# The split of a gate-up group's last pair on GpSimd, its products by lower parts at the end, and one more pair of FFN 1's second group as seven products

## The chip, the cores and the metric

The kernel runs on one core of a Trainium2 chip. The metric is the device time of one launch in microseconds (us). The engines in the text: TensorE (PE; its weight loads, which overlap the matmuls, are PEld), VectorE (DVE), ScalarE (ACT), GpSimd (POOL) and SyncE (SP), which issues most of the DMAs.

## The reference, cut to what matters

One encoder layer on x (256 tokens x 2048): two SwiGLU feed-forward networks with a mixer between them, all in float32. Each FFN is

```
def swiglu(x, w_gate_up, w_down):
    gate, up = jnp.split(x @ w_gate_up, 2, axis=-1)
    return (jax.nn.silu(gate) * up) @ w_down
```

with w_gate_up 2048 x 11264 and w_down 5632 x 2048. The change touches only the first product of both FFNs, `x @ w_gate_up`.

## The kernel before, in words

**Two parts of a number.** Every float32 operand is split in an upper part h (a cast to the matmul type, on ACT, line 176) and a lower part l = value - h (a subtraction, on DVE unless another engine is given, line 177). A product is three matmuls, h by h, h by l and l by h, each with a stationary 128x128 piece of x and a moving 128x512 piece of the weights (`three`, line 443).

**Groups and pairs.** The gate-up product runs over 11 groups g (512 gate columns and 512 up columns); a group runs over 8 pairs u of 128 rows of x. Its result is four PSUM banks c[m][n] (m: half of the tokens, n: gate or up). A plain pair is 8 products, so 24 matmuls. A pair in `MIXED_IN` is done as seven products, 21 matmuls, by a scheme of sums: sums of the blocks of x are made once, and sums of the blocks of w for every group (`splits`, lines 985 and 986, with a DMA that adds one part of w to another, `add_second`, line 148, on GpSimd's queue). The first of its four blocks is split ahead by `prepare`, as h1 and l1. The seven products go to four more banks p1, p5, p6, p7 besides the c banks. In groups 2 to 10 of both networks the pairs 2, 4, 5 and 6 are done so; in group 1, a network's second, only 4 and 5 in FFN 1 and 2, 4 and 5 in FFN 2; in group 0 none.

**The boundary.** At the end of a group the p banks have to be added into the c banks. `boundary` does it while PE works on the last pair, 7: ACT copies p1 (L1193), and then DVE does a row of eight instructions: L1194 adds to c[0][0], L1195 and L1196 take in p6 and p7, L1197 adds to c[1][0], L1200 and L1201 lead to c[0][1], L1203 and L1204 to c[1][1]. PE's products of pair 7 for a bank come behind the addition into that bank; the banks' order is (0,0), (1,0), (0,1), (1,1). p6 is made in pair 6, whose seven products are in the order p1, c[0][0], p5, p7, p6, c[1][0], c[0][1].

**What sets the order.** The whole stage is written out by hand (`manual_schedule`): each engine takes its instructions in the order of the code, and waits at semaphores. `first_pairs` does pairs 0 and 1, `pair_ahead` pairs 2 to 5 (the splits of pair u+1 stand ahead of the products of pair u), and the loop at the end of `ffn` pairs 6 and 7. `units` does silu(gate)*up of the group that has ended (L1110, L1115), turns it on PE (L1135) and splits the result. Weights come by SP into five buffers; a buffer is loaded anew when its last split is done (`load_next`). In the kernel before GpSimd makes the lower parts of the next group's pair 0 (`boundary(g, gated.splits(g + 1, 0, nc.gpsimd))`), besides the adding DMAs.

In the names of the trace `xt` is x in its two parts, `xs` the sums of its blocks, `raw` the weights as they come, `pa` and `pb` the PSUM banks (c[0][.], p1, p5 are pa; c[1][.], p6, p7 are pb), and `z` and `s` two rooms of 128x512.

## Time and profile before

| | |
|---|---|
| median of three runs | 1807.68 us (1807.27 to 1808.6) |
| the profiled execution's own time | 1807.96 us |
| its span, first to last instruction | 1806.1 us |
| granted TensorE clock | 0.999 |
| PE busy | 1794.5 us (99%), 8368 matmuls |
| DVE busy | 1618.9 us (90%) |
| ACT busy | 1130.3 us (63%) |
| POOL busy | 214.8 us (12%) |

The profile's rows give, for an instruction or a run of like ones, the start from the span's begin, the duration, engine, line, operation, what it writes and reads, and in brackets the idle time before it with what ended it. A matmul's start is recorded and its end is modelled, so matmuls that follow each other overlap in the rows; their rate is read from start to start. One of a group's windows, by the times of its rows, is 172.56 to 214.36 us: from the first matmul of FFN 1's pair 7 in group 3 to that in group 4.

### The profile page before, as it was taken

What the parts mean: (1) busy time and instruction counts of PE and PEld (TensorE: products, weight loads), DVE (VectorE), ACT (ScalarE), POOL (GpSimd) and SP (SyncE); (2) the same over time, 40 slices, a digit from 0 to 9 for tenths busy, and PEclk for the clock granted to TensorE, in tenths of its full rate; (3) what the DMA queues carried; (4) which work ended last, traced back from release to release, by engine and by line L of the source; (5) the groups of instructions that cost most, each with busy time, mean ns of one, the idle gap of its engine ahead of it and who ended that gap; (6) DMA issues with size and microseconds to landing.
All of it is one profiled execution on the core that took longest, in us unless ns stands there. A gap on an engine that the chain in (4) does not pass through costs nothing.

```text
span 1806.1 us, 23876 instructions
## 1 busy us (share of the span) xinstructions
PE 1794.5 (99%) x8368; PEld 1491.2 (83%) x8368; DVE 1618.9 (90%) x2114; ACT 1130.3 (63%) x1487; POOL 214.8 (12%) x194
## 2 busy tenths in 40 slices
PE   9999999999999999999999999999999999999998
PEld 7888888888888888888889888888888888888886
DVE  6999999888999999888888888898999988899997
ACT  7566666655656667566667666556666566566663
POOL 0022211111000100000000000011111222000010
PEclk9999999999999999999999999999999999999999
DMA  9788988887799996954555767889888888699994
GB/s 370 232 253 278 285 280 255 257 248 217 249 328 305 309 285 244 293 157 166 177 168 170 253 200 273 246 239 277 279 269 276 256 249 256 188 318 339 277 315 165
DMA packets 128023, 460.63 MB, mean 255 GB/s; under 512 B 14352, under 2 KB 17168, under 8 KB 126368
## 3 DMA queue, kind: packets, MB, share of 16 engines
q1 hardware_dynamic: 109152, 391.18, 60.5%
q0 software_dynamic: 18608, 67.68, 20.6%
q8 instruction: 65, 1.06, 0.2%
q14 instruction: 54, 0.44, 0.1%
q10 hardware_dynamic: 144, 0.26, 0.0%
HBM read 444.38 MB, written 14.68 MB: 254 GB/s over the span
## 4 chain that ended last, share of the span: by engine, by line
PE 94%; DVE 3%; DMA 1%; ACT 1%; issue 1%; SPq 0%; POOL 0%; DVEq 0%; ACTq 0%
PE pa L443 44%; PE pb L443 38%; PE pa L315 6%; PE pa L320 3%; DVE l L177 1%; DMA raw<-in_w_mix_in_dram 1%; PE pb L1766 1%; PE pb L1135 1%; PE pa L1135 1%; PE pa L369 0%; PE pa L368 0%; PE pa L367 0%; PE pb L2065 0%; ACT xt L227 0%; ACT h L176 0%
## 5 line engine op out<-in xcount | busy, mean ns | idle before, releaser
L176 ACT CAST h<-raw 128x1024 fp32r<-128x1024 f32 (+1 forms) x849 | 831.3, 1009 | 431.6 <-PE pb L443 145.1
L177 DVE TENSOR_TENSOR l<-raw,h 128x1024 fp32r<-128x1024 f32 (+1 forms) x813 | 920.9, 1165 | 105.1 <-ACT h L176 86.8
L443 PE MATMUL pa<-h,xt 128*128 128x512 f32 x1198 | 420.6, 392 | 0.2 <-DVE xt L232 0.2
L443 PE MATMUL pb<-h,xt 128*128 128x512 f32 x1044 | 372.9, 391 | 0.4 <-DVE pb L1197 0.4
L443 PEld LDWEIGHTS pa<-h,xt 128*128 128x128 f32 x1198 | 225.0, 188 | 48.9 <-DVE xt L232 0.6
L443 PEld LDWEIGHTS pb<-h,xt 128*128 128x128 f32 x1044 | 195.9, 188 | 46.6 <-DVE pb L1204 4.0
L443 PE MATMUL pa<-l,xt 128*128 128x512 f32 x599 | 233.7, 390 | 0.6 <-DVE l L177 0.6
L443 PE MATMUL pb<-l,xt 128*128 128x512 f32 x522 | 203.3, 389 | 0.0
L443 PE MATMUL pb<-h,ht 128*128 128x512 f32 x428 | 151.2, 389 | 0.0
L443 PE MATMUL pa<-h,ht 128*128 128x512 f32 x428 | 151.1, 389 | 0.0
L148 POOL DMA_DIRECT2D raw<-in_w_ffn_gate_up_dram x77 | 67.2, 872 | 679.9 <-DVE l L177 623.8
L443 PEld LDWEIGHTS pa<-l,xt 128*128 128x128 f32 x599 | 112.6, 188 | 23.4 <-DVE l L177 1.3
L443 PE MATMUL pa<-h,xs 128*128 128x512 f32 x328 | 117.2, 389 | 0.0
L443 PE MATMUL pb<-h,xs 128*128 128x512 f32 x328 | 114.3, 389 | 0.0
L443 PEld LDWEIGHTS pb<-l,xt 128*128 128x128 f32 x522 | 98.1, 188 | 18.9
L315 PE MATMUL pa<-xt,h 128*128 128x512 f32 x448 | 109.9, 393 | 0.0
L315 PEld LDWEIGHTS pa<-xt,h 128*128 128x128 f32 x448 | 81.5, 188 | 15.3
L443 PEld LDWEIGHTS pa<-h,ht 128*128 128x128 f32 x428 | 80.4, 188 | 16.6
L443 PEld LDWEIGHTS pb<-h,ht 128*128 128x128 f32 x428 | 80.3, 188 | 16.6
L177 POOL TENSOR_TENSOR l<-raw,h 128x1024 fp32r<-128x1024 f32 x36 | 91.5, 2725 | 0.0
L443 PE MATMUL pa<-l,ht 128*128 128x512 f32 x214 | 83.3, 389 | 0.0
L443 PE MATMUL pb<-l,ht 128*128 128x512 f32 x214 | 83.3, 389 | 0.0
(341 smaller groups left out, 2592.4 us busy)
## 6 DMA issues: line engine op xcount, KB each, us to landing
raw<-in_w_ffn_gate_up_dram SPq DMA_DIRECT2D x350, 512.0 KB, 6.3
raw<-in_w_ffn_down_dram SPq DMA_DIRECT2D x176, 512.0 KB, 8.5
raw<-in_w_mix_in_dram SPq DMA_DIRECT2D x94, 512.0 KB, 4.8
raw<-in_w_ffn_gate_up_dram POOLq DMA_DIRECT2D x77, 512.0 KB, 8.4
raw<-in_w_ffn_down_dram POOLq DMA_DIRECT2D x42, 512.0 KB, 8.8
ht<-away SPq DMA_DIRECT2D x24, 512.0 KB, 10.7
raw<-in_w_mix_out_dram SPq DMA_DIRECT2D x24, 512.0 KB, 5.6
away<-ht SPq DMA_DIRECT2D x16, 512.0 KB, 7.4
```

The lines of the kernel that those rows point to most:

```text
L148: nc.gpsimd.dma_start(raw[:, 0:1024], src[:, 512:1536], accum_op=ALU.add)
L176: nc.scalar.copy(hi, src)
L177: by.tensor_tensor(lo, src, hi.bitcast(F32), ALU.subtract)
L315: nc.tensor.matmul(slot[f], weights(hs, kk, f), xcol(xt, k), start=(k == 0), stop=(k == KT - 1))
L320: nc.tensor.matmul(slot[f][:, 0:T], weights(ls, kk, f), xcol(xt, kh * 8 + kk, 0), start=False, stop=False,)
L443: nc.tensor.matmul(self.bank(at), lhs, rhs, start=(n == 1), stop=n in (ends, self.of[at]), skip_group_check=n > ends,)
L1135: nc.tensor.transpose(bank[:, o : o + P], zs[m][:, k * P : (k + 1) * P], ident)
L1766: nc.tensor.matmul(dst, left[a], right[b], start=first and i == 0, stop=last and i == 2)
```

## The change

The boundary's last pair is taken in another way. Until now a bank got all of its six matmuls of pair 7 (two rows of blocks, three matmuls each) before the next bank. Now (`take_parted`) a bank gets the four that use upper parts of the weights, and the eight that use lower parts, two for each bank, come at the very end (`lower`). The row of eight DVE instructions keeps its order, with new line numbers: L1193 is L1259, L1194 to L1197 are L1260 to L1263, L1200 and L1201 are L1266 and L1267, L1203 and L1204 are L1269 and L1270; L443 is L447, L985 and L986 are L1001 and L1002, L1110 and L1115 are L1176 and L1181.

GpSimd makes the lower parts of pair 7, behind a copy of one column (L1316) that waits for pair 6's last lower part, and the lower parts of the first blocks of the next group's pairs 4 and 5. DVE makes those of the next group's pair 0 again, behind the row of additions, and the first half of pair 1 then. The `prepare` of the next group's pair 2 moves from behind pair 7's splits to pair 5. In `units` DVE reads the turned bank in place of ACT's copy. In FFN 1's group 1 pair 6 is done as seven products too. A set `FIVE_IN` of groups with five such pairs is empty, so the code for it does nothing.

```diff
     def sums_of(u, w, also=None):
         also = u if also is None else also
         nc.vector.tensor_tensor(
-            w[:, S3::2, :], u[:, 0, :].rearrange("p (m t) -> p m t", m=2), u[:, :, P:T], ALU.subtract
+            w[:, S3::2, :], u[:, 0, :].rearrange("p (m t) -> p m t", m=2), also[:, :, P:T], ALU.subtract
         )
...
+    FIVE_IN = ()
...
-            some = MIXED_IN[1:3] if opened else MIXED_IN[:3]
+            some = MIXED_IN[1:] if opened else MIXED_IN[:3]
...
-        def prepare(self, g, u):
+        def prepare(self, g, u, by=nc.vector):
...
-            split_act(h, l, raw[:, 0:512])
+            split_act(h, l, raw[:, 0:512], by)
...
+        def take_parted(self, g, u):
+
+            (h0, l0), (h1, l1) = self.split_of.pop((g, u))
...
+            def upper(m, n):
+                for k in range(2):
+                    at, ah, al, h, _ = parts(m, n, k)
+                    self.some_of(at, (ah, h), (al, h))
+
+            def lower():
+                for k in range(2):
+                    for n in range(2):
+                        for m in range(2):
+                            at, ah, _, _, l = parts(m, n, k)
+                            self.some_of(at, (ah, l))
+
+            return upper, lower
...
             def boundary(g, ahead):
...
-                rest_of = gated.take(g, last)
-
-                def bank(m, n):
-                    for k in range(2):
-                        rest_of[4 * k + 2 * m + n]()
+                bank, lower = gated.take_parted(g, last)
...
                 bank(1, 1)
+                lower()
                 some(ahead, 2)
...
-            def first_pairs(g, waiting):
+            def first_pairs(g, waiting, ahead):
...
+                if ahead:
+                    some(waiting, 2)
+                    gated.prepare(g, sevens[1], nc.gpsimd)
+                    some(ahead, 1)
...
             def pair_ahead(g, u):
...
                 for one in gated.take(g, u):
                     one()
+                if u == last - 2 and g < NG - 1:
+                    gated.prepare(g + 1, MIXED_IN[0])
                 for _ in ahead:
                     pass
+                if u == last - 2:
+                    done = gated.split_of[g, last - 1][-1][1]
+                    nc.gpsimd.tensor_copy(warm[:, 2:3], done[:, 0:1].bitcast(F32))
...
-                    some(gated.splits(g, last), 2)
-                    if g < NG - 1:
-                        gated.prepare(g + 1, MIXED_IN[0])
+                    some(gated.splits(g, last, nc.gpsimd), 2)
                     for one in gated.take(g, last - 1):
                         one()
-                    boundary(g, gated.splits(g + 1, 0, nc.gpsimd) if g < NG - 1 else splits(0))
-                    waiting = units(gated.c, rest)
+                    boundary(g, gated.splits(g + 1, 0) if g < NG - 1 else splits(0))
+                    if g < NG - 1:
+                        begun = gated.splits(g + 1, 1)
+                        next(begun)
+                    among = None
+                    if g < NG - 1:
+                        third = (FIVE if g + 1 in FIVE_IN else MIXED_IN)[2]
+                        among = lambda g=g, u=third: gated.prepare(g + 1, u, nc.gpsimd)
+                    waiting = units(gated.c, rest, among)
                     some(waiting, 2)
```

The rows below show the order at three places of FFN 1's group 3. The names carry a number that differs between the two kernels; `h_1540`, `l_1541`, `h_1544`, `l_1545` are pair 7's parts before, and `h_1556`, `l_1557`, `h_1560`, `l_1561` those in the change; `xt_125` is x. A bracket names the engine whose semaphore a row waits for.

PE before, at the end of pair 7, bank c[1][1] (pb_1274) and the start of the next group (pa_1625):

```order
L443 MATMUL pa_1272<-l_1545,xt_125 128x512
L443 MATMUL pa_1272<-h_1544,xt_125 128x512
L443 MATMUL pb_1274<-h_1540,xt_125 128x512 [waits DVE_49]
L443 MATMUL pb_1274<-l_1541,xt_125 128x512
L443 MATMUL pb_1274<-h_1540,xt_125 128x512
L443 MATMUL pb_1274<-h_1544,xt_125 128x512
L443 MATMUL pb_1274<-l_1545,xt_125 128x512
L443 MATMUL pb_1274<-h_1544,xt_125 128x512
L443 MATMUL pa_1625<-h_1611,xt_124 128x512 [waits Activation_49]
```

PE at the same place in the change, bank c[1][1] is pb_1288 and the next group begins with pa_1640:

```order
L447 MATMUL pb_1288<-h_1556,xt_125 128x512 [waits DVE_49]
L447 MATMUL pb_1288<-h_1556,xt_125 128x512
L447 MATMUL pb_1288<-h_1560,xt_125 128x512 x2
L447 MATMUL pa_1285<-l_1557,xt_125 128x512 [waits Pool_49]
L447 MATMUL pb_1287<-l_1557,xt_125 128x512
L447 MATMUL pa_1286<-l_1557,xt_125 128x512
L447 MATMUL pb_1288<-l_1557,xt_125 128x512
L447 MATMUL pa_1285<-l_1561,xt_125 128x512 [waits Pool_49]
L447 MATMUL pb_1287<-l_1561,xt_125 128x512
L447 MATMUL pa_1286<-l_1561,xt_125 128x512
L447 MATMUL pb_1288<-l_1561,xt_125 128x512
L447 MATMUL pa_1640<-h_1622,xt_124 128x512 [waits Activation_49]
```

Behind the wait for the last addition stood six matmuls of the group; now four and the eight by lower parts stand there, twelve.

DVE before, from pair 6's last split (l_1531) to the additions; l_1541 and l_1545 are pair 7's, l_271_1551 is the first block of the next group's pair 2:

```order
L177 TENSOR_TENSOR l_1531<-raw_489,h_1530 128x1024 [waits Activation_49]
L177 TENSOR_TENSOR l_1541<-raw_486,h_1540 128x1024 [waits DMAHW4_49,Activation_49]
L177 TENSOR_TENSOR l_1545<-raw_486,h_1544 128x1024 [waits DMAHW5_49,Activation_49]
L177 TENSOR_TENSOR l_271_1551<-raw_492,h_270_1550 128x512 [waits DMAHW6_49,Activation_49]
L1194 TENSOR_TENSOR pa_1271<-pa_1271,z_1576 128x512 [waits PE_49,Activation_49]
L1195 TENSOR_TENSOR s_1577<-pb_1394,z_1576 128x512 [waits PE_49]
```

DVE in the change; l_1546 is pair 6's last split, l_267_1541 the first block of the next group's pair 2:

```order
L177 TENSOR_TENSOR l_1516<-raw_489,h_1515 128x1024 [waits Activation_49]
L177 TENSOR_TENSOR l_267_1541<-raw_492,h_266_1540 128x512 [waits DMAHW6_49,Activation_49]
L177 TENSOR_TENSOR l_1546<-raw_489,h_1545 128x1024 [waits Activation_49]
L1260 TENSOR_TENSOR pa_1285<-pa_1285,z_1587 128x512 [waits PE_49,Activation_49]
L1261 TENSOR_TENSOR s_1588<-pb_1404,z_1587 128x512 [waits PE_49]
```

Two splits of pair 7 no longer stand ahead of the additions; the row that takes in p6 (pb_1394 before, pb_1404 now) waits for PE in both.

GpSimd in the change, from the copy that waits for pair 6's last split to the adding DMA of the next group's pair 5 (before, the two splits that stood there, l_1612 and l_1616, were those of the next group's pair 0):

```order
L1316 COPY warm<-l_1546 128x1 [waits DVE_49]
L177 TENSOR_TENSOR l_1557<-raw_486,h_1556 128x1024 [waits DMAHW4_49,Activation_49]
L177 TENSOR_TENSOR l_1561<-raw_486,h_1560 128x1024 [waits DMAHW5_49,Activation_49]
L177 TENSOR_TENSOR l_291_1647<-raw_483,h_290_1646 128x512 [waits DMAHW2_49,Activation_49]
L148 DMA raw_483<-in_w_ffn_gate_up_dram 128x1024 [waits DMASW5_49,Pool_49]
L177 TENSOR_TENSOR l_305_1716<-raw_486,h_304_1715 128x512 [waits DMAHW0_49,PE_49,Activation_49]
L148 DMA raw_486<-in_w_ffn_gate_up_dram 128x1024 [waits DMASW6_49,Pool_49]
```

The adding DMAs of pairs 4 and 5 now stand behind two more instructions on GpSimd's queue.

## The prediction

> **What bounds the kernel now.** I read the busy table first, then the window of one whole group, then PE's and DVE's timelines around one boundary of groups, because the change is repeated there twenty times (groups 1 to 10, two networks).

> ```profile
> PE 1794.5 (99%) x8368; PEld 1491.2 (83%) x8368; DVE 1618.9 (90%) x2114; ACT 1130.3 (63%) x1487; POOL 214.8 (12%) x194
> ```

> The profiled execution's own time is 1807.96 us, 1.9 above its span of 1806.1 and 0.28 above the median of the runs shown (1807.68). In a group's window (span; then busy time of PE, PEld, DVE, ACT, POOL) PE has no idle time:

> ```profile
> 172.56:214.36 41.80, 41.80 (x190) 34.45 (x188) 38.02 (x46) 26.09 (x31) 8.25 (x7) 1.00 0.90 280
> ```

> 180 matmuls of 512 columns and eight transposes stand in such a group. So a PE wait lengthens the kernel by itself, and DVE has 41.80 - 38.02 = 3.8 us to spare per group. The boundary of group 3 on PE (start, duration, what):

> ```profile
> 170.97 0.39 PE L443 MATMUL pb<-h,xs 128*128 128x512 f32 x1
> ...
> 172.56 0.39 PE L443 MATMUL pa<-h,xt 128*128 128x512 f32 x1
> ...
> 173.92 0.39 PE L443 MATMUL pb<-h,xt 128*128 128x512 f32 x1
> ...
> 176.67 0.45 PE L443 MATMUL pb<-h,xt 128*128 128x512 f32 x1
> 176.96 0.40 PE L443 MATMUL pb<-l,xt 128*128 128x512 f32 x1
> ...
> 178.10 0.39 PE L443 MATMUL pa<-h,xt 128*128 128x512 f32 x1
> ```

> 170.97 is the last matmul of p6. 172.56 begins pair 7, 173.92 its second bank: six matmuls in 1.36 us, 0.227 each. 176.67 begins the last bank c[1][1]; its first matmul takes 0.29 to the next, 0.06 too long. 178.10 begins the next group. DVE meanwhile:

> ```profile
> 168.03 2.96 DVE L177 TENSOR_TENSOR l<-raw,h 128x1024 fp32r<-128x1024 f32 x3
> 170.90 0.69 DVE L1194 TENSOR_TENSOR pa<-pa,z 128x512 f32<-128x512 f32 x1
> 171.50 0.68 DVE L1195 TENSOR_TENSOR s<-pb,z 128x512 f32<-128x512 f32 x1
> ...
> 175.87 0.70 DVE L1204 TENSOR_TENSOR pb<-pb,s 128x512 f32<-128x512 f32 x1
> ```

> The first row is pair 7's two splits (1.14 each, start to start) and a half-sized one (0.68). Then come the eight additions, which end at 175.87 + 0.70 = 176.57. The last bank's first matmul, put right by its 0.06, begins at 176.73: 0.16 after the addition it waits for. So two rows of work end together here: PE's 18 matmuls for three banks and DVE's additions. The kernel is bound by PE, and DVE's row of additions is just level with it at each boundary.

> **The change part by part.** *The order of pair 7's matmuls.* Ahead of the last bank PE now has 12 matmuls instead of 18, so it would be there at 172.56 + 12 x 0.227 = 175.28, while the addition is over at about 176.5: PE waits. Behind the wait stand 4 + 8 = 12 matmuls instead of 6. The same matmuls are done, but 6 x 0.227 = 1.36 us of them lie behind the wait that lay ahead of it.

> *Can the additions begin earlier?* Two of DVE's splits ahead of them are gone, so one must know what would hold them next. Group 10 shows it, where the half-sized split is missing before too:

> ```profile
> 463.57 0.39 PE L443 MATMUL pb<-h,xs 128*128 128x512 f32 x1
> ...
> 470.65 0.39 PE L443 MATMUL pa<-h,ht 128*128 128x512 f32 x1
> ```

> ```profile
> 464.00 0.69 DVE L1195 TENSOR_TENSOR s<-pb,z 128x512 f32<-128x512 f32 x1 [0.41 <-PE pb L443]
> ...
> 468.37 0.70 DVE L1204 TENSOR_TENSOR pb<-pb,s 128x512 f32<-128x512 f32 x1
> ```

> There DVE stood idle for 0.41 us, and L1195 began 0.43 after the start of p6's last matmul: it cannot begin before. In group 3 that is 170.97 + 0.43 = 171.40, against 171.50 now. All that DVE is relieved of brings 0.10 us. p6's place among pair 6's products is not changed.

> *Sum for a boundary of groups 2 to 9.* End of additions 176.47, last bank 0.16 later at 176.63, twelve matmuls (2.72) to 179.35, against 178.10: +1.25 us. The waits ahead of the other banks are inside that, since the last one ends last. Sixteen boundaries: 20.0 us. In group 10 the additions end at 468.37 + 0.70 = 469.07 as before; + 0.16 + 2.72 = 471.95 against 470.65: +1.30, twice 2.6 us.

> *Group 1 of FFN 1*, where pair 6 becomes seven products:

> ```profile
> 84.41 2.96 DVE L177 TENSOR_TENSOR l<-raw,h 128x1024 fp32r<-128x1024 f32 x3 [0.26 <-ACT h L176]
> 87.29 0.69 DVE L1194 TENSOR_TENSOR pa<-pa,z 128x512 f32<-128x512 f32 x1
> ...
> 92.26 0.70 DVE L1204 TENSOR_TENSOR pb<-pb,s 128x512 f32<-128x512 f32 x1
> ```

> ```profile
> 90.16 0.50 PE L443 MATMUL pb<-h,xt 128*128 128x512 f32 x1 [0.40 <-DVE pb L1197]
> ...
> 94.50 0.39 PE L443 MATMUL pa<-h,xt 128*128 128x512 f32 x1
> ```

> Here DVE is late already and PE waits for it. Three matmuls fewer (0.68) buy nothing then; DVE's work counts. It gains a half-sized split (0.60 start to start), two sums of w and one full split for pair 6, and loses pair 7's two splits:

> ```profile
> L985 DVE TENSOR_TENSOR raw<-raw 128x512 f32<-128x512 f32 x77 | 53.4, 693 | 2.6
> ```

> 0.60 + 2 x 0.72 (0.69 and a step of 0.03) - 1.14 = +0.9; the wait of 0.26 for ACT goes with pair 7's splits, so I take +0.6: L1204's successor ends at 93.56, and 93.56 + 0.16 + 2.72 = 96.44 against 94.50: +1.9 (bounds 1.3 and 3.0: DVE not later at all, or 1.7 later, should the three go the other way).

> *Group 1 of FFN 2*, where pair 6 stays plain and p6 is early:

> ```profile
> 1188.80 0.61 PE L443 MATMUL pa<-h,xt 128*128 128x512 f32 x2
> ...
> 1196.87 0.39 PE L443 MATMUL pa<-h,xt 128*128 128x512 f32 x1
> ```

> ```profile
> 1189.66 0.69 DVE L1194 TENSOR_TENSOR pa<-pa,z 128x512 f32<-128x512 f32 x1
> ...
> 1194.62 0.70 DVE L1204 TENSOR_TENSOR pb<-pb,s 128x512 f32<-128x512 f32 x1
> ```

> The first addition needs c[0][0]'s last matmul of pair 6, at 1188.80, + 0.43 = 1189.23: 0.43 earlier than now, no more. End 1194.89, + 2.88 = 1197.77 against 1196.87: +0.9.

> *GpSimd's lower parts.* Its full split, and the two beside the additions of group 3:

> ```profile
> L177 POOL TENSOR_TENSOR l<-raw,h 128x1024 fp32r<-128x1024 f32 x36 | 91.5, 2725 | 0.0
> ```

> ```profile
> 171.91 5.08 POOL L177 TENSOR_TENSOR l<-raw,h 128x1024 fp32r<-128x1024 f32 x2
> ```

> Pair 7's two may begin when pair 6's last split is done (DVE's splits of pair 6 end at 168.1, and 0.6 later with the half-sized one now ahead): 168.7 + 2 x 2.73 = 174.2. PE wants them at 177.5 and 178.4, behind its wait: hidden with 4 us to spare. The half-sized split on GpSimd is in no row; between DVE's 0.68 and the full 2.73 I take half, 1.4. Each holds the adding DMA behind it on GpSimd's queue back by that much; I take it as hidden, since the sums that read it are due about two pairs (10 us) later, and what is at stake if not is 1.4 us for one such DMA. DVE's splits of the next pair 0 (2.3 us) and the half of pair 1 now stand behind the additions, ahead of L1115: the next group's first split is ready by 176.47 + 1.2 = 177.7, before PE's 179.35, and the transposes that want L1115's result stand behind pair 0 (5.4 us). Cost 0. SP's reload of pair 7's buffer waits for GpSimd now, some 4 us later; its data are wanted half a group later. Cost 0.

> L1204 takes 0.70 at 175.87, beside GpSimd's splits, and 0.70 at 468.37 in group 10, without them: the additions are not slowed. [...]

> *Sum:* 20.0 + 2.6 + 1.9 + 0.9 = +25.4 us on 1807.96, 1833.4; against the median **1833 us**, 1.4% slower.

> **The rivals.** *The additions are level again* (faster): if they began 1.25 us sooner, at 170.15, no bank would wait, and what is left is 0.68 us of matmuls, the wait of 0.40 in FFN 1's group 1 and 0.06 at each of 18 boundaries: about -2.2, 1805.5. For it speaks that DVE is relieved of 2.3 us ahead of them; against it, that p6's last matmul starts only at 170.97. The same time would come if PE did the products by lower parts during the wait; a wait such as the 0.40 before 90.16 says it holds what is behind. Chance 0.03.

> *No difference* (about 1807.7): the wait takes back exactly what other places gain; those are the 0.68 + 0.40 + 18 x 0.06 = 2.2 us of the first rival at most, so this needs the waits at 18 boundaries to be under 0.1 us. Chance 0.02.

> *Half as dear*: the additions get faster or are released earlier, 0.6 us a boundary: +13, 1821. From L1195 on they take 5.07 us in groups 3 and 10 alike (171.50 to 176.57, 464.00 to 469.07), so nothing points to it. Chance 0.04.

> *GpSimd late as well*: pair 7's lower parts at twice their time would end at 168.7 + 10.9 = 179.6, 1.2 us after PE wants the second: +1.2 at each boundary, 1857. It decides from 4.2 us of delay. Against it: all 36 splits on GpSimd stood beside such additions and took 2.73 on the mean, and no split of DVE's runs beside these two. [...] Chance 0.06.

> **How the numbers follow.** The forecast has 0.85. Its own bounds are +-0.15 us at each of 18 boundaries (the two lags, 0.43 and 0.16, are each read from one place), 2.7 us; below, FFN 1's group 1 at 1.3 and FFN 2's at nothing, another 1.5; above, FFN 1's group 1 at 3.0 and one adding DMA late, another 2.5: 1828 to 1838. That leaves out the rivals, 0.15 together, and I keep it as the range. 0.2% (3.6 us) is about what a measurement of this kernel can tell from no change. Faster 0.03, same 0.02, slower 0.95.

> **What would show it.** In the profile of the changed kernel: a group of 43.05 us between its first matmuls instead of 41.80; PE idle ahead of three banks of pair 7, by 0.3, 0.5 and 0.55 us, ended by L1263, L1267 and L1270, at every boundary; L1261 0.43 after p6's last matmul; GpSimd's splits over before L1270 is; DVE's busy share lower. I am wrong if a group still takes 41.8 us, if those waits end with another releaser, or if PE waits elsewhere, for GpSimd or a DMA.

## The result and the profile after

The changed kernel takes 1837.9 us (median of 4 runs, 1837.34 to 1838.84) against 1807.54 us (4 runs) for the kernel before: a ratio of 1.0167, interval 1.0150 to 1.0185, so 30.4 us slower. The forecast was 1833 us, in a range of 1828 to 1838.

The busy table of the changed kernel's page, to be held against that of before:

```profile
PE 1812.0 (99%) x8365; PEld 1490.8 (81%) x8365; DVE 1603.7 (87%) x2078; ACT 1129.6 (61%) x1489; POOL 275.5 (15%) x255
```

PE is still "99% busy" with three matmuls fewer, and the kernel is 31 us longer. Most of the time of the waits does not show as idle time. A matmul's row lasts 0.39 us, to its modelled end, while the next one starts 0.227 us after it where nothing is waited for, so the first 0.16 us or so of a wait are covered. And the four matmuls behind a wait take 1.19 or 1.20 us in the rows, in place of 1.07. The starts tell the whole of it. The window of a whole group, from the first matmul of group 3's pair 7 to that of group 4's:

```profile
179.42:222.51 43.09, 42.59 (x189) 34.39 (x189) 37.13 (x44) 25.88 (x31) 11.04 (x10) 1.00 0.89 268
```

43.09 us instead of 41.80; 43.05 was forecast. PE's rows at that boundary, from p6's last matmul on:

```profile
177.89 0.39 PE L447 MATMUL pb<-h,xs 128*128 128x512 f32 x1
...
179.48 1.07 PE L447 MATMUL pa<-h,xt 128*128 128x512 f32 x4
180.59 1.19 PE L447 MATMUL pb<-h,xt 128*128 128x512 f32 x4
181.98 1.20 PE L447 MATMUL pa<-h,xt 128*128 128x512 f32 x4 [0.20 <-DVE pa L1267]
183.44 1.19 PE L447 MATMUL pb<-h,xt 128*128 128x512 f32 x4 [0.26 <-DVE pb L1270]
184.47 0.40 PE L447 MATMUL pa<-l,xt 128*128 128x512 f32 x1
...
186.30 0.39 PE L447 MATMUL pa<-h,xt 128*128 128x512 f32 x1
```

Four matmuls take 4 x 0.227 = 0.91 us, but the banks start 1.11, 1.39 and 1.46 apart: waits of 0.20, 0.48 and 0.55 us, where the brackets show nothing, 0.20 and 0.26. From the last bank's first matmul to the next group (186.30) are 2.86 us, for twelve matmuls. DVE and then GpSimd at the same place:

```profile
176.53 0.70 DVE L1260 TENSOR_TENSOR pa<-pa,z 128x512 f32<-128x512 f32 x1 [1.05 <-ACT z L1259]
178.32 0.69 DVE L1261 TENSOR_TENSOR s<-pb,z 128x512 f32<-128x512 f32 x1 [1.09 <-PE pb L447]
...
182.69 0.70 DVE L1270 TENSOR_TENSOR pb<-pb,s 128x512 f32<-128x512 f32 x1
183.29 3.48 DVE L177 TENSOR_TENSOR l<-raw,h 128x1024 fp32r<-128x1024 f32 x3
```

```profile
175.54 0.21 POOL L1316 COPY warm<-l 128x1 f32<-128x1 f32 x1
175.69 4.78 POOL L177 TENSOR_TENSOR l<-raw,h 128x1024 fp32r<-128x1024 f32 x2
```

DVE now stands idle for 1.05 and 1.09 us ahead of its additions: the time it was relieved of is not used. L1261 begins 178.32 - 177.89 = 0.43 us after p6's last matmul, and the last addition is over at 183.39. GpSimd has both lower parts at 180.47, 4.0 us before PE takes the first (184.47).

FFN 1's group 1 went worse than forecast. PE there:

```profile
90.57 1.21 PE L447 MATMUL pa<-h,xt 128*128 128x512 f32 x4 [2.66 <-DVE pa L1260]
92.69 2.08 PE L447 MATMUL pb<-h,xt 128*128 128x512 f32 x4 [0.90 <-DVE pb L1263]
94.56 1.91 PE L447 MATMUL pa<-h,xt 128*128 128x512 f32 x4
96.27 1.91 PE L447 MATMUL pb<-h,xt 128*128 128x512 f32 x4
97.97 0.63 PE L447 MATMUL pa<-l,xt 128*128 128x512 f32 x1
```

Two long waits, and behind them 1.71 us for four matmuls (94.56 to 96.27): 0.427 each, about half the usual rate. The next group's first matmul starts at 100.12, against 94.50 before. What stood ahead of L1260, on ACT and on DVE:

```profile
86.79 0.62 ACT L176 CAST xs<-s 128x512 fp32r<-128x512 f32 x1 [3.46 <-DVE s L399]
87.31 1.99 ACT L176 CAST h<-raw 128x1024 fp32r<-128x1024 f32 x2
89.21 0.57 ACT L1259 COPY z<-pa 128x512 f32<-128x512 f32 x1
```

```profile
84.96 0.68 DVE L1150 TENSOR_TENSOR z<-xt 128x512 f32<-128x512 f32 x1
...
87.44 0.69 DVE L177 TENSOR_TENSOR xs<-s,xs 128x512 fp32r<-128x512 f32 x1 [0.69 <-ACT xs L176]
89.81 0.70 DVE L1260 TENSOR_TENSOR pa<-pa,z 128x512 f32<-128x512 f32 x1 [1.68 <-ACT z L1259]
...
94.78 0.70 DVE L1270 TENSOR_TENSOR pb<-pb,s 128x512 f32<-128x512 f32 x1
```

ACT's copy of p1 (L1259) stands in ACT's queue behind the rounding of `xs`, the sums of x for pair 2 of the next group, and behind two casts of pair 7's weights, which come after that rounding. Those sums DVE makes from L1150 on, behind pair 6's sums of the weights. The eight additions then wait 1.68 us for that copy.

### The profile page after: what moved, and what is told of

Read it like the earlier page. It is cut to its first block, busy times and chain, and to the rows that moved or that the text cites. A ratio compares the mean times of both kernels' runs of the same rounds, so it can differ in the third digit from the quotient of the medians.

```text
span 1837.1 us, 23983 instructions
## 1 busy us (share of the span) xinstructions
PE 1812.0 (99%) x8365; PEld 1490.8 (81%) x8365; DVE 1603.7 (87%) x2078; ACT 1129.6 (61%) x1489; POOL 275.5 (15%) x255
## 4 chain that ended last, share of the span: by engine, by line
PE 87%; DVE 8%; DMA 2%; issue 1%; ACT 1%; SPq 0%; POOL 0%; DVEq 0%; ACTq 0%
PE pa L447 39%; PE pb L447 34%; PE pa L315 6%; PE pa L320 3%; DVE l L177 1%; DMA raw<-in_w_ffn_gate_up_dram 1%; DVE z L1262 1%; DVE pb L1263 1%; DVE s L1261 1%; PE pa L369 1%; DVE pa L1267 1%; DVE pb L1270 1%; DVE s L1269 1%; PE pa L368 1%; PE pa L367 1%
## 5 line engine op out<-in xcount | busy, mean ns | idle before, releaser
L176 ACT CAST h<-raw 128x1024 fp32r<-128x1024 f32 (+1 forms) x851 | 836.2, 1009 | 455.7 <-PE pb L447 143.2
L177 DVE TENSOR_TENSOR l<-raw,h 128x1024 fp32r<-128x1024 f32 (+1 forms) x775 | 902.5, 1191 | 110.3 <-ACT h L176 89.0
L447 PE MATMUL pa<-h,xt 128*128 128x512 f32 x1194 | 409.3, 394 | 6.5 <-DVE pa L1267 3.6
L447 PE MATMUL pb<-h,xt 128*128 128x512 f32 x1038 | 362.9, 396 | 6.8 <-DVE pb L1270 5.0
L447 PEld LDWEIGHTS pa<-h,xt 128*128 128x128 f32 x1194 | 223.3, 188 | 60.4 <-DVE pa L1267 11.9
L447 PEld LDWEIGHTS pb<-h,xt 128*128 128x128 f32 x1038 | 192.9, 189 | 61.7 <-DVE pb L1270 13.3
L447 PE MATMUL pa<-l,xt 128*128 128x512 f32 x597 | 233.3, 391 | 0.1
L447 PE MATMUL pb<-l,xt 128*128 128x512 f32 x519 | 202.2, 390 | 0.0
L177 POOL TENSOR_TENSOR l<-raw,h 128x1024 fp32r<-128x1024 f32 (+1 forms) x76 | 142.7, 1897 | 227.9 <-ACT h L176 227.9
L447 PE MATMUL pb<-h,ht 128*128 128x512 f32 x428 | 151.2, 389 | 0.0
L447 PE MATMUL pa<-h,ht 128*128 128x512 f32 x428 | 151.1, 389 | 0.0
L447 PEld LDWEIGHTS pa<-l,xt 128*128 128x128 f32 x597 | 112.4, 188 | 24.2 <-DVE l L177 1.4
L447 PE MATMUL pa<-h,xs 128*128 128x512 f32 x332 | 119.0, 389 | 0.8 <-DVE sums L399 0.8
L447 PE MATMUL pb<-h,xs 128*128 128x512 f32 x332 | 115.7, 389 | 0.0
L447 PEld LDWEIGHTS pb<-l,xt 128*128 128x128 f32 x519 | 97.6, 188 | 20.4
L447 PEld LDWEIGHTS pb<-h,ht 128*128 128x128 f32 x428 | 80.3, 188 | 16.7
L447 PEld LDWEIGHTS pa<-h,ht 128*128 128x128 f32 x428 | 80.3, 188 | 16.6
L148 POOL DMA_DIRECT2D raw<-in_w_ffn_down_dram x42 | 36.5, 868 | 350.0 <-DVE la L177 289.0
L447 PE MATMUL pa<-l,ht 128*128 128x512 f32 x214 | 83.3, 389 | 0.0
```

Of the source, the lines that this page charges most:

```text
L148: nc.gpsimd.dma_start(raw[:, 0:1024], src[:, 512:1536], accum_op=ALU.add)
L176: nc.scalar.copy(hi, src)
L177: by.tensor_tensor(lo, src, hi.bitcast(F32), ALU.subtract)
L447: nc.tensor.matmul(self.bank(at), lhs, rhs, start=(n == 1), stop=n in (ends, self.of[at]), skip_group_check=n > ends,)
```

## The experiments

**Theory A**, the prediction's: PE waits at each boundary for DVE's row of additions, which p6 releases, and what the change costs is that six more of PE's matmuls lie behind the last wait. **Theory B**, the rival that blames GpSimd: its splits are late, or in DVE's way.

### The order alone

The kernel before, with only pair 7's order changed (the splits stay on DVE):

```
-                rest_of = gated.take(g, last)
+                bank, lower = gated.take_parted(g, last)
...
                 bank(1, 1)
+                lower()
```

> The kernel before, with the new order of pair 7's matmuls alone; every split stays on the engine that had it. Theory A (PE waits for DVE's row of additions, and 12 matmuls instead of 6 stand behind that wait): the additions keep their times, 5.07 us from L1195's successor to the end, and each group takes 1.25 us more: 18 boundaries by 1.25 and two group-1 boundaries by 1.34, together 25, so 1832 to 1833 us. Theory B (GpSimd's splits of pair 7 cost the time, being late or in DVE's way): no change, 1807 to 1809 us.

Measured: 1835.15 us, ratio 1.0149 (1.0134 to 1.0165), 27.2 us slower. PE and the first and last addition in group 3:

```profile
176.46 1.20 PE L446 MATMUL pb<-h,xt 128*128 128x512 f32 x4
177.85 1.20 PE L446 MATMUL pa<-h,xt 128*128 128x512 f32 x4 [0.20 <-DVE pa L1226]
179.31 1.20 PE L446 MATMUL pb<-h,xt 128*128 128x512 f32 x4 [0.26 <-DVE pb L1229]
```

```profile
174.19 0.68 DVE L1220 TENSOR_TENSOR s<-pb,z 128x512 f32<-128x512 f32 x1
...
178.55 0.70 DVE L1229 TENSOR_TENSOR pb<-pb,s 128x512 f32<-128x512 f32 x1
```

The same waits with the same releasers, and none of pair 7's work on GpSimd. Theory B is out for the bulk of the time. A group takes 1.37 us more. That is 0.12 over the 1.25 expected, which makes the 2 us by which the run missed 1833, and 0.09 over the changed kernel's 1.28: 0.09 us is all that taking pair 7's splits off DVE is worth at a boundary.

### The lower parts among the banks

The changed kernel with its eight late products spread, five matmuls for c[0][0] ahead of c[1][0], then seven, six and six:

```
                 bank(0, 0)
+                lower((0, 0, 0))
                 bank(1, 0)
+                lower((1, 0, 0), (0, 0, 1), (1, 0, 1))
...
                 bank(0, 1)
+                lower((0, 1, 0), (0, 1, 1))
...
                 bank(1, 1)
-                lower()
+                lower((1, 1, 0), (1, 1, 1))
```

> The changed kernel, with the eight products by lower parts put among the banks, so that 18 matmuls of pair 7 stand ahead of the last bank again and 6 behind its wait; all splits stay on GpSimd. Theory A: the waits ahead of c[0][1] and c[1][1] go, a group takes 41.80 us again; 18 boundaries by 1.28, FFN 2's group 1 by 1.4 and FFN 1's by 0.6 are won: about 1813 us, the rest over 1808 being FFN 1's group 1. Theory B: GpSimd's splits are as they were, so no more than 3 us are won, 1835 to 1838 us.

Measured: 1812.31 us, ratio 1.0024 (1.0015 to 1.0034); 25.6 us of the 30.4 are back. A group's window:

```profile
175.59:217.40 41.81, 41.81 (x190) 34.53 (x189) 37.61 (x44) 25.97 (x31) 11.76 (x10) 1.00 0.91 277
```

41.81 us, with GpSimd's splits as in the changed kernel. In groups 2 to 10 the change of order is the cost, and the splits on GpSimd are not. Of what is left over the kernel before, 3.5 us arise in FFN 1's group 1 and 0.7 in FFN 2's, by this run's trace.

### p6 sooner, twice

If p6 releases the additions, making it sooner must help with all else alike. First p6 and p7 ahead of p5, then c[1][0] ahead of p5 as well:

```
-... (0, 1, 3, 4, 5, 6, 2) if before_fold ...
+... (0, 1, 5, 4, 3, 6, 2) if before_fold ...
```

```
-... (0, 1, 3, 4, 5, 6, 2) if before_fold ...
+... (0, 1, 5, 4, 6, 3, 2) if before_fold ...
```

> The changed kernel, with pair 6's seven products in the order p1, c[0][0], p6, p7, p5, c[1][0], c[0][1]: p6 is made 6 matmuls (1.36 us) sooner, and nothing else moves. Theory A: L1261 is released by p6; it starts 1.2 us sooner (then L1260 ahead of it holds it, which waits for ACT's copy of p1), so the waits ahead of pair 7's banks shrink by 1.15 us in 18 groups: about 1817 us; FFN 1's group 1, where L1260 is late itself, stays. Theory B: 1837 to 1838 us, no change.

> The changed kernel with pair 6's seven products in the order p1, c[0][0], p6, p7, c[1][0], p5, c[0][1]. In the run with p5 ahead of c[1][0] the additions began 1.2 us sooner, but L1263 then waited 0.38 us for c[1][0]'s own last product, and p5 isn't read before L1266. Theory A: that wait goes, the last addition ends 1.2 us sooner than in the changed kernel, 0.34 us more is won in 18 groups than in that run: 1815.5 us. If something else held the additions back there, the time stays at 1821 us.

Measured: 1821.62 us for the first (ratio 1.0075, 1.0060 to 1.0090), 1818.31 for the second (1.0059, 1.0042 to 1.0075). DVE in group 3 of the first:

```profile
174.25 0.70 DVE L1260 TENSOR_TENSOR pa<-pa,z 128x512 f32<-128x512 f32 x1 [1.05 <-ACT z L1259]
174.86 0.68 DVE L1261 TENSOR_TENSOR s<-pb,z 128x512 f32<-128x512 f32 x1
...
176.72 0.70 DVE L1263 TENSOR_TENSOR pb<-pb,z 128x512 f32<-128x512 f32 x1 [0.38 <-PE pb L447]
```

The row begins sooner and gains 0.85 us per group, not the 1.15 expected, since a new wait of 0.38 stands inside it: L1263 adds to c[1][0], whose own product of pair 6 I had pushed behind p5. In the second run that wait is gone and 0.27 us more per group is won (0.34 was expected), 1.1 of 1.28. So the release by p6 is shown, and with it that the additions are a chain in which a later step can have a product of its own to wait for. 1815.5 was expected of the second; the median is 2.8 us higher, and its profiled execution, at 1816.2, is nearer. What differs between executions is told at the end.

### FFN 1's group 1

Pair 6 plain again there, and, apart from it, the sums of x for the next group's pair 2 moved from group 1 into group 2:

```
-            some = MIXED_IN[1:] if opened else MIXED_IN[:3]
+            some = MIXED_IN[1:3] if opened else MIXED_IN[:3]
```

```
-                if g == 1 and u in sums_at:
+                if g == 1 and u in sums_at and not (opening and u == 5):
                     sums_in(sums_at[u])
...
                 for one in gated.take(g, 0):
                     one()
+                if opening and g == 2:
+                    sums_in(MIXED_IN[0])
```

> The changed kernel, with FFN 1's group 1 as before (pair 6 plain, pairs 4 and 5 as seven products). Theory A1 (in that group the sums for pair 6 hold DVE and ACT back, ACT's copy of p1 stands behind them, and PE's long wait is followed by a stretch of matmuls at half rate): the group's cost falls from 5.4 to about 0.5 us, 1833 us, and no matmul of that group is 0.43 us from the next. Theory A2 (the prediction's step, DVE 0.6 us later for it): 1.4 us won, 1836.5 us.

> The changed kernel, with one thing moved in FFN 1: the sums of x for pair 2, made in group 1 behind pair 5's products, are made in group 2 behind pair 0's products. Theory A1 (in group 1 ACT's copy of p1 and with it DVE's additions stood behind the rounding of these sums, and DVE behind pair 6's sums of the weights reached them late): the additions begin 0.43 us after p6's last matmul, 3.8 us sooner; PE's waits of 2.66 and 0.90 us and the matmuls at half rate go, 5.4 us are won: 1832.4 us. Theory A3 (the seven products of pair 6 themselves leave PE short of work there, whatever DVE's order): less than 1 us is won, 1837 us.

Measured: 1834.21 us (ratio 1.0143, 1.0128 to 1.0158) with pair 6 plain, 3.7 us won. In the trace the first transposition behind that boundary starts 4.7 us sooner, and no matmul there is at half rate: the size that A1 had, not A2's 1.4. But DVE's wait for ACT's copy is still there:

```profile
86.81 0.70 DVE L1260 TENSOR_TENSOR pa<-pa,z 128x512 f32<-128x512 f32 x1 [1.70 <-ACT z L1259]
```

So this run took away DVE's work for pair 6 and not the wait; the next one shortens the wait, to 0.70 us. With the sums moved the kernel took 1836.92 us (1.0159, 1.0144 to 1.0174), only 1.0 won. Yet in group 1 that run went as A1 said. DVE in group 1, then the place in group 2 that the sums were moved to, and PE there:

```profile
85.83 0.70 DVE L1260 TENSOR_TENSOR pa<-pa,z 128x512 f32<-128x512 f32 x1 [0.70 <-ACT z L1259]
86.68 0.69 DVE L1261 TENSOR_TENSOR s<-pb,z 128x512 f32<-128x512 f32 x1
```

```profile
101.09 0.69 DVE L1150 TENSOR_TENSOR z<-xt 128x512 f32<-128x512 f32 x1 [2.65 <-PE pb L1201]
...
103.65 0.69 DVE L177 TENSOR_TENSOR xs<-s,xs 128x512 fp32r<-128x512 f32 x1 [0.69 <-ACT xs L176]
```

```profile
111.43 0.47 PE L447 MATMUL pa<-h,xs 128*128 128x512 f32 x1 [2.77 <-DVE sums L399]
```

The additions begin 3.74 us sooner (86.68 against 90.42), and group 2 begins at 94.68 instead of 100.12: 5.4 us, as forecast. Then they are lost in group 2. The sums use the room `z`, which PE's transpositions (L1201) still read, so DVE waits 2.65 us and all its work behind that comes late. PE waits 2.77 us at pair 2, and seven matmuls behind that start 0.427 apart. What ends PE's wait is L399, DVE's last reading of the turned bank. The code has four `pa` banks, and c[0][0], c[0][1], p1 and p5 need them all, so p5's product has to wait until the turned bank has been read. A1 holds for group 1; moved work took its wait along.

### All mended, and a fifth pair as seven products

Both edits together, the order of the banks and the sums moved:

> The changed kernel with both edits, the products by lower parts among the banks and the sums of pair 2 later. Theory A: no wait is left at any boundary and FFN 1's group 1 is 0.7 us shorter than in the kernel before: 1808.5 us, the same as before, 29 us under the changed kernel.

1811.7 us (1.0019, 1.0010 to 1.0029): the 2.77 us in group 2 are there as above, the boundaries are level. The 1808.5 expected had not counted that stall. So the next run keeps the order of the banks, has pair 6 plain in place of the moved sums, and takes the split of the next group's pair 4 back to DVE (`gated.prepare(g, sevens[1])`):

> The changed kernel with the products by lower parts among the banks, FFN 1's group 1 with pair 6 plain, and the half-sized split of the next group's pair 4 on DVE again. Theory A: no boundary waits any more and nothing holds FFN 1's group 1 or 2: 1808 to 1809 us, no different from the kernel before. In the run with both edits that half-sized split on GpSimd (2.04 us) and a full one of DVE's (2.31 us) held each other up; here DVE's takes 1.22 us again, which moves no time, since DVE has room.

1807.78 us, ratio 1.0000 (0.9991 to 1.0010). A group of it:

```profile
173.24:215.05 41.81, 41.81 (x189) 34.54 (x188) 37.22 (x44) 26.07 (x30) 9.69 (x8) 1.00 0.91 275
```

DVE has 0.8 us per group less to do than before (37.22 for 38.02), PE's time is what it was: the relief by itself buys nothing. It could be spent on fewer matmuls, with `FIVE_IN = range(3, 11)` on either of the last two kernels:

> The kernel with both edits, and the code for a fifth pair as seven products used: pair 3 too in groups 3 to 10 of both networks. Three matmuls (0.68 us) fewer in 16 groups; DVE gets 3.2 us more per group (a half-sized and a full split, two sums), on about 37.5 of 41.1. Theory A, if DVE's time left holds it: 10.9 us won on the kernel with both edits, about 1798 us. If DVE's order is too tight, its additions begin late and a group is as long as DVE's row: between 1800 and 1815 us.

> The kernel of the run before this one, with pair 3 as seven products in groups 3 to 10 of both networks. If what made the first run with a fifth pair slow was DVE's loss beside GpSimd's half-sized split (1.1 us in each group, 0.5 us net of the split that DVE now makes itself) and the stall in FFN 1's group 2: 16 by 0.5 and 3 us less than its 1821, 1810 us. If DVE's row is full in any case, 1815 us or more. Theory A gives 1798 us only if DVE has nothing late at all.

On the first kernel 1820.98 us (1.0072, 1.0055 to 1.0089). That is above both answers, and 9.3 us more than the same kernel without the fifth pair: by the trace its 16 groups take 0.5 us more than before on the mean. On the second kernel 1807.55 us (0.9999, 0.9989 to 1.0008), near the first answer, 1810. 48 matmuls fewer are 10.9 us less for PE, and no time is won. A group of the second kernel:

```profile
168.97:211.00 42.03, 41.74 (x187) 33.90 (x186) 40.07 (x49) 27.31 (x34) 10.78 (x11) 1.00 0.96 288
```

Three matmuls fewer, and this group is longer (42.03 for 41.81), with DVE at 40.07. PE waits at the boundary again. By its rows it is idle for 0.25 us ahead of c[1][0], until DVE's addition is done. Then, by the starts, it waits 0.22 us for GpSimd's second split of pair 7, which ends at 174.01 and is taken at 174.06: with the lower parts among the banks, GpSimd is no longer hidden here. The 16 groups are not alike. From transposition to transposition they take 41.1 to 42.7 us, and in sum as long as before to 0.2 us; what makes them differ stays open. No version here beats the kernel before by more than a measurement can tell.

### One more split on GpSimd

The half-sized split of pair 6's first block too, beside DVE's own splits (`gated.prepare(g, MIXED_IN[3], nc.gpsimd)`):

> The changed kernel, with one more half-sized split per group on GpSimd, that of the first block of pair 6, which falls beside DVE's own splits. Theory A: DVE's full splits beside it take 1.14 to 1.23 us as elsewhere and the time stays at 1838 us, since DVE is not what ends last there. If GpSimd and DVE contend where both operands are in SBUF, DVE's splits beside it take clearly longer than 1.23 us (up to 1.3 us more), and the half-sized one on GpSimd over 1.31.

1836.25 us (1.0157, 1.0136 to 1.0177): no slower, and groups 2 to 10 are as in the changed kernel. But the splits do hold each other up. GpSimd and DVE in group 4:

```profile
198.63 1.81 POOL L177 TENSOR_TENSOR l<-raw,h 128x512 fp32r<-128x512 f32 x1 [1.70 <-ACT h L176]
```

```profile
198.05 1.23 DVE L177 TENSOR_TENSOR l<-raw,h 128x1024 fp32r<-128x1024 f32 x1 [0.97 <-ACT h L176]
200.09 1.42 DVE L177 TENSOR_TENSOR l<-raw,h 128x1024 fp32r<-128x1024 f32 x1 [0.82 <-ACT h L176]
```

GpSimd's begins while DVE's runs to 199.28 and ends 1.16 us after that; DVE's next begins while GpSimd's runs to 200.44 and ends 1.07 us after that. Each takes, from the end of the other's, 0.15 us less than it takes alone (1.31 and 1.23): by these times it has waited, and not run slowly. The second of my two answers is right on the mechanism, and on its size the loss here is 0.2 us for DVE and 0.5 for GpSimd.

## Why the prediction was right, and where it was off

| boundary | forecast | measured |
|---|---|---|
| groups 2 to 9, both networks (16) | 16 x 1.25 = 20.0 | 16 x 1.28 = 20.5 |
| group 10 (2) | 2 x 1.30 = 2.6 | 1.37 + 1.33 = 2.7 |
| FFN 1, group 1 | 1.9 | 5.4 |
| FFN 2, group 1 | 0.9 | 1.0 |
| FFN 2, group 1's pair 2 | 0 | 1.4 |
| FFN 1, ahead of group 1 | 0 | 0.2 |
| between the two networks | 0 | -0.5 |
| sum | 25.4 | 30.7 |

The measured column is how much later the first transposition behind each boundary starts (L1135 before, L1201 after), less what the row ahead had already brought; in FFN 2's group 1 the first matmul of pair 7 parts the two rows. The last two rows are not the change's: against the kernel before they lie between -0.3 and 0.3 us and between -0.5 and 0.5 in the traces of the other kernels.

The measured time lies 0.1 us inside the range, and that is luck. The group 1 of both networks together took 5.0 us more than forecast, where 1.1 had been allowed for. What covers the rest is room meant for other things: 2.7 us for 18 boundaries, which needed 0.6, and 1.4 for a late adding DMA, which no wait of PE in the trace is for.

*The order of pair 7's matmuls*: right, and shown by the run with the order alone and by the one with the lower parts among the banks. *Additions can't begin earlier*: right, to the 0.43 us, and shown by both runs with p6 sooner. The 0.10 us of relief is 0.09. *GpSimd hidden*: right; a half-sized split takes 1.30 us (1.4 was taken), a full one 2.43 (2.73). DVE's loss beside the half-sized split is there and hidden: two full splits from 188.57 on, with GpSimd's running to 188.98, take 2.62 us instead of 2.35, once per group. *The rivals*: the first said the same time would come if PE did products by lower parts during the wait. PE did not do so by itself: in group 3 it waited 0.55 us ahead of c[1][1], to 183.44, with both lower parts ready from 180.47, and took the first product by them at 184.47, where the code has it. With that order written out a group is level again, at 41.81 us, which is the time of before and not the 1805.5 us of that rival.

*Group 1 of FFN 1* is the step that failed. "DVE's work counts" gave the end of the additions as 93.56; it was 95.48. I added DVE's instructions and left out ACT's queue, where L1259 stands behind the rounding of the sums. DVE's idle 1.68 us for it, and the 0.2 by which PE was late ahead of group 1, make the difference to within 0.1. From 95.48, 0.16 + 2.72 lead to 98.36; the group began at 100.12, the other 1.76 us being the matmuls at half rate, which no row of before had shown behind a wait. The bounds of 1.3 and 3.0 were too narrow for both. The half rate differs between executions: in the run with one more split on GpSimd the clock was halved for half as long, and this group cost 4.2 us.

*Group 1 of FFN 2*: the boundary is right to 0.1 us. What failed is a cost put at nothing, that of DVE's new order behind the boundary. PE waits at pair 2's products, where it did not before. PE and DVE in the change, and DVE's like row before:

```profile
1185.99 0.47 PE L447 MATMUL pa<-h,xs 128*128 128x512 f32 x1 [0.84 <-DVE sums L399]
```

```profile
1185.55 0.29 DVE L399 TENSOR_TENSOR sums<-pa,sums 128x128 f32<-128x128 f32 x1
```

```profile
1166.49 0.29 DVE L398 TENSOR_TENSOR sums<-z,sums 128x128 f32<-128x128 f32 x1
```

Before, these sums read `z`, ACT's copy, and the turned bank was free early; now DVE reads the bank itself and holds it, as in the run with the sums moved. L399 also comes 2.3 us later against the transposition. One full split more stands ahead of it, and at the transposition DVE was 1.1 us further behind PE already. No run takes these apart, and the wait is not in every trace: in the run with one more split on GpSimd this group as a whole cost 1.1 us.

## What to carry to other kernels

Work that is moved from ahead of a wait to behind it adds its own time, since nothing then fills the wait (1.28 us a group here, for six matmuls of 0.227): count the matmuls ahead of the last wait and behind it, and look for what releases the chain before relieving the engine that runs it. Where an engine's row is made longer, walk every in-order queue that the row waits on, ACT's copies too (1.68 us of DVE's time here). A copy that is saved can cost a wait elsewhere: the bank is then held until its later reader is done (PE waited 0.84 us for it in FFN 2's group 1). In this kernel the helper engine bought nothing (0.09 us a boundary), because the engine that it helped was not what ended last.

## What the runs showed of the hardware

**PE at half rate.** In the changed kernel matmuls from 93.28 to 98.40 start 0.427 us apart, and the granted clock is halved meanwhile. The clock is the third number from the end of a row, PE's busy time the one behind the comma. First the changed kernel, then the first run with p6 sooner, then the second:

```profile
88.37:91.79 3.42, 1.21 (x4) 0.67 (x4) 1.94 (x3) 3.42 (x5) 3.35 (x2) 1.00 0.69 211
91.79:95.20 3.41, 2.51 (x6) 2.04 (x7) 3.13 (x6) 0.83 (x1) 1.34 (x1) 0.50 0.70 215
95.20:98.61 3.41, 3.41 (x9) 2.65 (x9) 3.41 (x4) 0.00 (x0) 0.00 (x0) 0.50 0.54 155
```

```profile
88.98:92.40 3.42, 1.19 (x4) 0.67 (x4) 2.63 (x5) 3.38 (x5) 3.42 (x2) 1.00 0.69 213
92.40:95.81 3.41, 3.31 (x8) 2.63 (x9) 3.24 (x6) 0.00 (x0) 0.47 (x1) 0.50 0.71 228
```

```profile
86.52:89.93 3.41, 1.69 (x8) 1.07 (x6) 1.17 (x2) 3.41 (x5) 1.85 (x1) 1.00 0.96 233
89.93:93.35 3.42, 2.15 (x8) 1.35 (x8) 3.11 (x6) 2.33 (x3) 2.85 (x2) 1.00 0.58 182
```

So waits of this length bring the half rate in some executions and not in others: behind PE's wait of 2.77 us in the run with both edits, to 109.97, the matmuls start 0.227 us apart from 110.28 on. The half rate cost 0.2 us (0.427 for 0.227) for each of 12 matmuls in the changed kernel. That fits the third kernel's runs: 1816.2 us at a mean clock of 0.999 (the profiled one), and 1818.2 to 1818.6 at 0.997 to 0.998.

**Splits on DVE and GpSimd hold each other up.** A larger case is in the run with both edits, where GpSimd's half-sized split and two full ones of DVE's meet in every group. GpSimd, then DVE:

```profile
92.90 2.04 POOL L177 TENSOR_TENSOR l<-raw,h 128x512 fp32r<-128x512 f32 x1 [3.01 <-ACT h L176]
```

```profile
92.58 3.44 DVE L177 TENSOR_TENSOR l<-raw,h 128x1024 fp32r<-128x1024 f32 x2
```

2.04 instead of 1.30, and 3.44 for two that take 2.35 elsewhere: GpSimd gave DVE no time, it took 1.1 us of DVE's to save it 0.68. The additions, with one operand in PSUM, kept their 5.07 us beside GpSimd's full splits (178.32 to 183.39 in the changed kernel, as from 464.00 to 469.07 before, without them).
